# A hybrid decoder layer on one core: loads issued some steps ahead of their use, and a region of its own for the group statistics

## The chip, the core and the metric

The kernel runs on one core of a Trainium2 chip. The metric is the device time of one execution in microseconds, of which the median of several runs is compared. The engines are TensorE (PE, matmuls; its weight loads are PEld), VectorE (DVE), ScalarE (ACT), GpSimd (POOL) and SyncE (SP, which only issues transfers). Each engine works through its own list of instructions in order.

## What is computed

One layer of a decoder over 2048 prompt tokens and 32 sample tokens (8 sequences of 4), all in float32 with width 1024. Cut to what matters, the reference is:

```python
def run_layer(x, bufs, ...):
    h = rms_norm(x, norm_pre_mix)
    q, k, v, z1, z2, g_a, g_b = project_inputs(h, w_in, b_gate)
    for gi, (win, dil) in enumerate(((128, 1), (512, 4), (2048, 16))):
        # prompt: window attention over every dil-th key; sample: the same over a cache
        o, lse = dilated_group_prompt(...) if bufs is None else dilated_group_sample(..., bufs[gi], ...)
    o_a = merge_dilations(outs, lses)       # softmax over the three groups' lse
    o_b = spatial_gate(z1, z2, ...)         # gMLP in chunks of 128
    merged = g_a * (o_a @ w_ao) + g_b * (o_b @ w_bo)
    x = x + rms_norm(merged @ w_out, norm_post_mix)
    h2 = rms_norm(x, norm_pre_ffn)
    f = jnp.square(jax.nn.relu(h2 @ w_up)) @ w_down
    return x + rms_norm(f, norm_post_ffn)
```

Each head group has four heads of 64; the kernel takes them as two pairs (hp 0 and 1).

## The kernel before

**Stages.** Half s = 0 holds 1024 prompt tokens and the 32 sample tokens, half s = 1 the other 1024 prompt tokens. For each half the program goes through six groups (pair hp, dilation g): `project` computes q, k and v of the group, `attention` its scores, values and statistics. After the three groups of a pair, `merge` weights their outputs. Then come `gmlp`, `mix` (gates and the branch outputs) and `out_rows` (the output projection, both norms, and the transposed h2). The feed-forward part `ffn` follows for both halves: each of its two products is done with seven block products in place of eight, for which sums of weight blocks (`weight_sums`) and differences of h2 quarters (`differences`) are made beforehand. Matmuls on float32 data take three passes over split operands (high and low parts `wh`, `wl`), so a weight block is loaded (L248), rounded on ACT (L264) and its remainder made on POOL (L267).

**Lanes.** The gemms of `project`, `gmlp`, `mix` and `out_rows` set the pace on TensorE. Between their matmuls they step generators in four lanes: lane 0 attention and norms, lane 1 merges, the moves of h2 and the differences, lane 2 the sample attention and what follows it, lane 3 `weight_sums`, stepped each time 12000 columns have gone by. A `yield` gives control back to the gemm. This order is the program's; on top of it the framework's scheduler, with a timeline of its own, orders each engine's instructions anew by readiness and priority, so the yields guide where an instruction stands but do not fix it. Transfers issued on SP with `tc.issue_after` stay behind the named load.

**What the change touches.**

`attention`: unit u's scores go through L648, which adds the mask and takes each row's minimum, and L652, which takes the exponential and its row sum. Both statistics are written into columns 128 to 131 of `uo`, the unit buffer that also holds the group's values and is stored to `us` in DRAM at the group's end (L724 to L733). There is one `uo` for all groups, in `ov`.

`merge`: for each of eight blocks of 128 tokens, `fetch` (L737) loads the three groups' rows of `us` one block ahead of use into `junk`; L751 to L763 make the weights, L765 and L766 add the groups on POOL, and after four blocks four transposes (L772) take the sum to `oa`.

`sample_attention`: for K and again for V, 21 pieces are loaded into a few buffers (`pieces`) on SP, 3 for group 0 and 9 for each other group: from the cache (L818, L825), and the new rows from `smp` (L828); q of each group by L843 into one buffer. For each piece VectorE does a product and a reduction (K: L846, L847) or a product and an addition (V: L877, L886), with sums on POOL (L887, L889). At the end a matmul against a constant (L893) sums over the partitions; for it POOL's L889 has to be done, and its result bank is tag "t", two banks that the transposes of other work also use. Pair hp = 0 runs beside the attention of s = 0, with three buffers, and pair hp = 1 beside `mix` of s = 0, with two.

`to_h2` and `moved`: a normed block is transposed, scaled on VectorE (L342) and stored to `h2` (L345); `differences` loads quarters of h2 (two transfers) and makes four differences on VectorE (L1208 to L1211).

`weight_sums`: per quarter of a weight, four SP transfers DRAM to DRAM (L1188) and four additions by transfers that accumulate, issued on POOL (L1191).

The names in the rows are the program's: `ps`, `pt`, `pg`, `pu` are banks of PSUM, `wh`/`wl` weights, `pair`, `flat`, `oa`, `act`, `ov`, `xt`, `junk`, `gbc`, `prod`, `zs`, `e0` buffers in SBUF, `us`, `smp`, `h`, `up_sums`, `down_sums` are in DRAM, `con` are constants.

Of the kernel before, what the change touches and what calls it, by code (L numbers as in the profile page):

```python
# [18 lines left out]
P = 128  # L19
D = 1024  # L20
# [74 lines left out]
def hybrid_step(ctx: ExitStack, tc: tile.TileContext, ins: dict, outs: list):  # L95
# [372 lines left out]
    count = {"s": 0, "t": 0, "q": 0}  # L468
# [110 lines left out]
    def attention(s, hp, g, idx, q, v):  # L579
# [26 lines left out]
        uo = units_of(ov[:, A_U : A_U + 8 * UW])  # L606

# [23 lines left out]
        def scores(u):  # L631
# [6 lines left out]
            for h in range(2):  # L638
                def keys(rows):
# [61 lines left out]
        for i in range(8 + LAG_T + LAG_V):  # L701
# [14 lines left out]
            if i == 7:  # L716
                k_used.add(idx)
        dst = us[s][hp][:, g, :]
# [12 lines left out]
    def merge(s, hp):  # L731
# [9 lines left out]
        yield  # L741
        for b4 in range(2):
# [25 lines left out]
            for _ in range(4):  # L768
                yield
# [11 lines left out]
    def sample_attention(hp):  # L781
# [9 lines left out]
        else:  # L791
# [4 lines left out]
            pieces = [a0[:, 0:512], a0[:, 512:1024]]  # L796
            prods = [sm.tile([P, 512], F32, tag="e0", name="prod") for _ in range(2)]
        cnt = [0, 0]

        def nxt(lst, w):  # L800
            cnt[w] += 1
            return lst[(cnt[w] - 1) % len(lst)]
# [3 lines left out]
        scv = sc.rearrange("p (e k) -> p e k", k=KEYS)  # L806

        def steps(kv):

            cs = slice(hp * P, hp * P + P)  # L810
            for g in range(3):
                while (hp, g) not in known:
                    yield None
                if g == 0:
                    src = cache[0][:, kv, cs].rearrange("(p i) c -> p i c", i=8)
                    for hf in range(2):
                        pc = t4(nxt(pieces, 0))
                        nc.sync.dma_start(pc, src[:, hf * 4 : hf * 4 + 4, :])  # L818
                        for i in range(4):
                            yield g, hf * 4 + i, pc[:, i, :].unsqueeze(1).to_broadcast([P, 4, P])  # L820
                else:
                    src = cache[g][:, kv, cs].rearrange("(p i r) c -> p i r c", i=8, r=DIL[g])
                    for i in range(8):
                        pc = t4(nxt(pieces, 0))
                        nc.sync.dma_start(pc, src[:, i, :4, :])  # L825
                        yield g, KEY0[g] + i, pc
                pc = nxt(pieces, 0)
                nc.sync.dma_start(pc, smp_d[g][hp][1 + kv].unsqueeze(1).to_broadcast([8, 16, 512]))  # L828
                pc = t4(pc)
                if g == 0:  # L830
                    for i in range(4):
                        yield g, 8 + i, pc[:, i, :].unsqueeze(1).to_broadcast([P, 4, P])
                else:
                    yield g, KEY0[g] + 8, pc

        loaded = -1
        for item in steps(0):
            if item is None:
                yield
                continue  # L840
            g, key, rows = item
            if g != loaded:
                nc.sync.dma_start(q, smp_d[g][hp][0].unsqueeze(1).to_broadcast([8, 16, 512]))  # L843
                loaded = g
            pr = nxt(prods, 1)
            nc.vector.tensor_tensor(t4(pr), t4(q), rows, ALU.mult)  # L846
            nc.vector.tensor_reduce(scv[:, :, key], hd(pr), AX, ALU.add)  # L847
            yield
# [26 lines left out]
        for n, (g, key, rows) in enumerate(steps(1)):  # L875
# [14 lines left out]
        yield  # L890
        yield
# [191 lines left out]
    def out_rows(s, behind=None):  # L1083
# [22 lines left out]

        def norms(b):
            y, n = of(b)
# [18 lines left out]
        def moved(b):  # L1127
            y, n = of(b)
            if s == 1:
                y = sm.tile([P, D], F32, tag="x", name="xt")  # L1130
                nc.sync.dma_start(y, n1_d[b * P : (b + 1) * P])
            for _ in range(5):
                yield
            yield from to_h2(s, y, n, b * P)
# [21 lines left out]
        for b in range(n_rows):  # L1156
            y, n = of(b)
            pt = gemm_rows([(list(zip(lhs(b), pb)), 256)], n)
            copy_any(y[:, 256:512], pt)
            pt = gemm_rows([(list(zip(lhs(b), w)), 512)], n)  # L1160
            free[0] = b + 1
            copy_any(y[:, 512:], pt)
            gen = push(0, norms(b))
            if s == 0:
                free[2] = push(1, after(gen, moved(b)))
            else:
                behind(b)
        if s == 1:
            drain(0)
            return [moved(b) for b in range(n_rows)] + [differences(s)]  # L1170
# [4 lines left out]
    def weight_sums():  # L1175

        for name, dst in (("w_up", up_d), ("w_down", down_d)):
            w = ins[name][0]
            hk, hm = w.shape[0] // 2, w.shape[1] // 2
            for q in range(4):  # L1180
                n = hk // 4
                rows = slice(q * n, (q + 1) * n)
                a11, a12 = w[q * n : (q + 1) * n, :hm], w[hk + q * n : hk + (q + 1) * n, :hm]
                a21, a22 = w[q * n : (q + 1) * n, hm:], w[hk + q * n : hk + (q + 1) * n, hm:]
                s1, s2, s3, s4 = (dst[i, rows] for i in range(4))
                for to, src in ((s1, a21), (s2, a11), (s3, a11), (s4, a12)):
                    with tc.issue_after(load[0].ins):
# [443 lines left out]
```

## Time and profile before

| | us |
|---|---|
| runs, median (lowest to highest) | 2965.51 (2965.22 to 2975.41) |
| profiled execution | 2969.44 |
| span of its profile | 2967.7 |

| engine | busy us | share |
|---|---|---|
| PE | 2854.4 | 96% |
| PEld | 2588.2 | 87% |
| DVE | 1323.3 | 45% |
| ACT | 1243.7 | 42% |
| POOL | 1185.7 | 40% |

The mean granted clock of TensorE is 0.983 of its full speed. To read it: TensorE is busy nearly all the time, its weight loads overlap its matmuls, and every other engine is idle more than half of the span. The shares are averages over stages. The rows that follow come from views by stretch of time and from the timelines of single engines. In a timeline row the number in brackets is the engine's idle time ahead of the instruction, with what ended it.

### The profile page before, as it was taken

The page shows a single profiled execution, that of the slowest core. Times are in us where ns is not written, and L with a number is a line of the kernel's source. Part 1 is how long each engine was busy: PE and PEld are TensorE (multiplying, and loading weights), DVE is VectorE, ACT ScalarE, POOL GpSimd, SP SyncE. Part 2 cuts the span into 40 slices and gives each one's busy share as a digit, 9 for nine tenths or more (in the row PEclk, how much of TensorE's full clock was granted, in tenths as well). Part 3 has the DMA queues.
Part 4 walks back from the last instruction along what each step waited for, and adds up shares of the span by engine and source line. Part 5 has one row for each costly group of instructions (what it writes and reads, how often), then busy time and mean ns, then how long its engine had stood idle before and what let it go on. Part 6 is the DMA issues. An engine that isn't in the chain of part 4 may idle for free. (4 is left out here: it accounts for less than half of the span.)

```text
span 2967.7 us, 45073 instructions
## 1 busy us (share of the span) xinstructions
PE 2854.4 (96%) x17382; PEld 2588.2 (87%) x17382; DVE 1323.3 (45%) x2288; ACT 1243.7 (42%) x2457; POOL 1185.7 (40%) x883
## 2 busy tenths in 40 slices
PE   8997999889998999999999999999999999999997
PEld 7897999889987888878889899999999888878885
DVE  5668456460473435451023654353343644452323
ACT  5353452211563434541134544554344555554343
POOL 3226224253302223143332344445555744445555
PEclk9998999999999999999999999999999999999998
DMA  5635525554459454353525987576665765686654
GB/s 166 187 117 167 155 71 143 139 147 120 135 184 234 134 146 117 83 127 91 145 81 200 301 277 236 180 244 213 206 197 191 241 205 187 192 275 191 192 182 149
DMA packets 463831, 515.50 MB, mean 174 GB/s; under 512 B 25472, under 2 KB 359872, under 8 KB 454400
## 3 DMA queue, kind: packets, MB, share of 16 engines
q1 hardware_dynamic: 452528, 475.59, 50.4%
q0 software_dynamic: 10944, 36.97, 6.9%
q8 instruction: 137, 2.24, 0.3%
q14 instruction: 78, 0.64, 0.1%
q10 hardware_dynamic: 144, 0.07, 0.0%
HBM read 396.96 MB, written 182.68 MB: 195 GB/s over the span
## 5 line engine op out<-in xcount | busy, mean ns | idle before, releaser
L283 PE MATMUL pg<-act,wh 128*128 128x352 f32 (+3 forms) x3424 | 948.8, 355 | 3.3 <-DVE xt L1055 1.4
L1241 POOL TENSOR_TENSOR wf<-raw,wf 128x512 fp32r<-128x512 f32 x448 | 633.2, 1416 | 688.2 <-ACT wf L1240 647.3
L283 PEld LDWEIGHTS pg<-act,wh 128*128 128x128 f32 x3424 | 617.3, 191 | 56.0 <-DVE xt L1055 2.4
L283 PE MATMUL pg<-act,wl 128*128 128x352 f32 (+3 forms) x1712 | 605.5, 354 | 0.0
L1240 ACT CAST wf<-raw 128x512 fp32r<-128x512 f32 x448 | 277.2, 619 | 505.0 <-PE pd L1330 205.0
L267 POOL TENSOR_TENSOR wl<-raw,wh 128x1024 fp32r<-128x1024 f32 (+1 forms) x106 | 253.5, 2392 | 386.2 <-ACT wh L264 334.6
L1330 PE MATMUL pd<-act,wf 128*128 128x264 f32 x2880 | 363.0, 286 | 7.4 <-ACT act L1240 4.6
L1330 PEld LDWEIGHTS pd<-act,wf 128*128 128x128 f32 x2880 | 356.5, 190 | 8.2 <-ACT act L1240 4.8
L283 PEld LDWEIGHTS pg<-act,wl 128*128 128x128 f32 x1712 | 326.5, 191 | 26.4
L1410 PE MATMUL pe<-wf,act 128*128 128x512 f32 x1008 | 237.1, 396 | 3.9 <-POOL wf L1241 3.9
L1410 PEld LDWEIGHTS pe<-wf,act 128*128 128x128 f32 x1008 | 190.3, 189 | 49.4 <-POOL wf L1241 4.7
L264 ACT CAST wh<-raw 128x1024 fp32r<-128x1024 f32 (+1 forms) x104 | 105.4, 1013 | 275.6 <-PE pg L283 155.3
L1339 DVE TENSOR_TENSOR ov<-pd,ov 128x528 f32<-128x528 f32 x140 | 96.2, 704 | 203.8 <-PE pd L1330 203.2
L1330 PE MATMUL pd<-pair,wf 128*128 128x264 f32 x1440 | 184.6, 284 | 0.0
L1330 PE MATMUL pe<-act,wf 128*128 128x512 f32 x768 | 182.6, 392 | 0.1
L1330 PEld LDWEIGHTS pd<-pair,wf 128*128 128x128 f32 x1440 | 178.1, 188 | 0.0
L1241 DVE TENSOR_TENSOR act<-flat,act 128x1024 fp32r<-128x1024 f32 (+1 forms) x76 | 103.1, 1360 | 158.7 <-ACT act L1240 158.6
L1330 PEld LDWEIGHTS pe<-act,wf 128*128 128x128 f32 x768 | 143.8, 188 | 32.9 <-ACT pair L1240 0.3
L652 ACT ACTIVATE ov<-ov 128x256 f32<-128x256 f32 (+1 forms) x192 | 91.8, 478 | 169.8 <-DVE ov L648 168.3
L1339 DVE TENSOR_TENSOR ov<-pe,ov 128x512 f32<-128x512 f32 x136 | 91.5, 687 | 137.3 <-PE pe L1330 126.4
L1330 PE MATMUL pd<-oa,wf 128*128 128x264 f32 x1056 | 135.0, 284 | 0.1
L1330 PEld LDWEIGHTS pd<-oa,wf 128*128 128x128 f32 x1056 | 130.9, 188 | 0.4 <-DVE oa L1241 0.3
(279 smaller groups left out, 4183.7 us busy)
## 6 DMA issues: line engine op xcount, KB each, us to landing
raw<-in_w_in_dram SPq DMA_DIRECT2D x84, 512.0 KB
raw<-up_sums SPq DMA_DIRECT2D x128, 256.0 KB
raw<-down_sums SPq DMA_DIRECT2D x128, 256.0 KB
flat<-f SPq DMA_DIRECT2D x48, 528.0 KB
raw<-in_w_up_dram SPq DMA_DIRECT2D x96, 256.0 KB
raw<-in_w_down_dram SPq DMA_DIRECT2D x96, 256.0 KB
flat<-f SPq DMA_DIRECT2D x48, 512.0 KB
f<-ov SPq DMA_DIRECT2D x16, 1056.0 KB
```

Of the source, the lines that this page charges most:

```text
L264: nc.scalar.copy(wh[:, :o], raw[:, :o])
L267: eng.tensor_tensor(wl[:, :o], raw[:, :o], wh[:, :o].bitcast(F32), ALU.subtract)
L283: nc.tensor.matmul(pt[:, :n], a[:, o : o + P], b, start=(i == 0 and j == 0), stop=(i == last and j == 2))
L652: nc.scalar.activation(pb[:, h, :w], pb[:, h, :w], AF.Exp, scale=-1.0, bias=uo[:, u, 128 + h : 129 + h], accum_out=uo[:, u, 130 + h : 131 ...
L1240: nc.scalar.copy(high, raw)
L1241: eng.tensor_tensor(low, raw, high.bitcast(F32), ALU.subtract)
L1330: nc.tensor.matmul(pt[:, o : o + n], w[:, a], x[:, b, c : c + n], start=first and j == 0, stop=last and j == 2)
L1339: nc.vector.tensor_tensor(X[to], res, X[add], ALU.add)
L1410: nc.tensor.matmul(pts[t], x[k][:, c, t * P : (t + 1) * P], w[:, d, 0], start=k == 0 and j == 0, stop=k == 15 and j == 2)
```

## The change

All changes are in how far ahead of its use data is asked for.

1. `attention` writes the row minima and sums to `stats`, a region of its own in `ov` with two buffers that take turns, and a GpSimd copy at step 9 puts them into `uo`. There are twelve such copies, one for each group of each half.
2. `merge` has four steps after its first fetch, two per block, and six ahead of the transposes (before: one, one, four).
3. `sample_attention` lists its loads and issues them as many pieces ahead as there are buffers; pair 1 has four buffers (two more in `ov`); q of group 1 has a buffer of its own; four steps stand ahead of the first use and five ahead of the last matmul (before: two).
4. `moved` is one generator over all blocks, paced by the norms, with two steps per half block.
5. `weight_sums` issues the loads of one quarter interleaved with the additions of the quarter before.
6. `differences` has four steps between load and use (before: one).

The core of the diff:

```diff
+    A_M = A_T + 1024
...
         uo = units_of(ov[:, A_U : A_U + 8 * UW])
+        stats = units_of(ring("m", A_M, 32, 2))
...
                     pb[:, h, :w], sp[:, h, :w], mask[:, 2 * P - w : 2 * P], 1.0, 3.0e38, ALU.add, ALU.min,
-                    uo[:, u, 128 + h : 129 + h],
+                    stats[:, u, h : h + 1],
...
-                    pb[:, h, :w], pb[:, h, :w], AF.Exp, scale=-1.0, bias=uo[:, u, 128 + h : 129 + h],
-                    accum_out=uo[:, u, 130 + h : 131 + h],
+                    pb[:, h, :w], pb[:, h, :w], AF.Exp, scale=-1.0, bias=stats[:, u, h : h + 1],
+                    accum_out=stats[:, u, 2 + h : 3 + h],
...
                 k_used.add(idx)
+            if i == 9:
+                nc.gpsimd.tensor_copy(uo[:, :, P:], stats)
...
         m3_next = fetch(0)
-        yield
+        for _ in range(4):
+            yield
...
                 yield
-            for _ in range(4):
+                yield
+            for _ in range(6):
                 yield
...
-            pieces = [a0[:, 0:512], a0[:, 512:1024]]
+            pieces = [a0[:, 0:512], a0[:, 512:1024], row(3)[:, 0:512], row(3)[:, 512:1024]]
...
+        qs = [q, U, q]
+        def load_q(g):
+            nc.sync.dma_start(qs[g], smp_d[g][hp][0].unsqueeze(1).to_broadcast([8, 16, 512]))
...
         def steps(kv):
+            todo, n = loads(kv), len(pieces)
+            issued = 0
+            for i, (g, _, shared, keys) in enumerate(todo):
+                while True:
+                    while issued < min(len(todo), i + n) and (hp, todo[issued][0]) in known:
+                        gi, src = todo[issued][:2]
+                        pc = pieces[issued % n]
+                        if kv == 0 and (issued == 0 or gi != todo[issued - 1][0]):
+                            load_q(gi)
+                        nc.sync.dma_start(t4(pc) if len(src.shape) == 3 and src.shape[2] == P else pc, src)
+                        issued += 1
+                    if issued > i:
+                        break
+                    yield None
+                if i == 0:
+                    for _ in range(4):
+                        yield None
+                pc = t4(pieces[i % n])
+                for j, key in enumerate(keys):
+                    yield g, key, pc[:, j, :].unsqueeze(1).to_broadcast([P, 4, P]) if shared else pc
...
-        yield
-        yield
+        for _ in range(5):
+            yield
         pu = ps.tile([P, 512], F32, tag="t", name="pt")
...
         def norms(b):
+            for _ in norm_steps(b):
+                paces[0] += 1
+                yield
...
-        def moved(b):
+        def moved():
+            for b in range(n_rows):
+                y, n = of(b)
+                if s == 1:
+                    y = sm.tile([P, D], F32, tag="x", name="xt")
+                    nc.sync.dma_start(y, n1_d[b * P : (b + 1) * P])
+                    for _ in range(4):
+                        yield
+                for _ in range(3):
+                    if paces[0] < 4 * (b + 1) + 2:
+                        yield
+                while paces[0] < 4 * (b + 1):
+                    yield
+                for _ in to_h2(s, y, n, b * P):
+                    yield
+                    yield
...
+            return ((s1, a21, a22), (s3, a11, a21), (s2, a11, s1), (s4, a12, s2))
+        before = None
+        for name, dst in (("w_up", up_d), ("w_down", down_d), (None, None)):
+            for q in range(4 if name else 1):
+                now = parts(name, dst, q) if name else None
+                for i in range(4):
+                    if now:
+                        with tc.issue_after(load[0].ins):
+                            nc.sync.dma_start(now[i][0], now[i][1])
+                        yield
+                    if before:
+                        nc.gpsimd.dma_start(before[i][0], before[i][2], accum_op=ALU.add, max_dma_last_dim=8192)
+                        yield
+                before = now
...
             nc.sync.dma_start(l, h2_d[s][k + 4])
-            yield
+            for _ in range(4):
+                yield
```

`loads(kv)` lists the transfers of the cache pieces and the new rows that stood in `steps` before, in the same sequence.

What the change does to the order of instructions stands here at three places. A row gives line, operation and what it writes from what it reads; lines of the changed program are some 2 to 40 higher.

VectorE, around the first scores of the second attention group of s = 0. Before, sample products (L846) and reductions (L847) stand ahead of the first score of the group (L648):

```order
L847 TENSOR_REDUCE xt<-ov 128x8 x2
L628 TENSOR_TENSOR oa<-flat_147,oa 64x256
L846 TENSOR_TENSOR ov<-xt,ov 128x512
L177 COPY ov<-pu 128x128
L847 TENSOR_REDUCE xt<-ov 128x8
L846 TENSOR_TENSOR ov<-xt 128x512
L846 TENSOR_TENSOR ov<-xt,ov 128x512
L847 TENSOR_REDUCE xt<-ov 128x8 x2
L522 COPY smp<-pg 128x32
L846 TENSOR_TENSOR ov<-xt,ov 128x512
L648 ISA ov<-ps,con 128x128
```

The same place of the changed program (L650 is the score, L858 the sample product, L561 a copy that stands five rows ahead of the piece above):

```order
L561 COPY st<-pt 32x384
L650 ISA ov<-ps,con 128x128
L650 ISA ov 128x1
L177 COPY ov<-pu 128x128
L177 COPY ov<-pt 128x512
L650 ISA ov<-ps,con 128x128
L650 ISA ov 128x1
L650 ISA ov<-ps,con 128x256
L650 ISA ov 128x1
L630 TENSOR_TENSOR oa<-flat_147,oa 64x256
L858 TENSOR_TENSOR ov<-xt 128x512
L858 TENSOR_TENSOR ov<-xt,ov 128x512
```

Three scores moved ahead of the sample products of this stretch.

SyncE, at the start of the sample attention of pair 1, before (L818 and L825 cache pieces, L828 new rows, L843 q, L248 weights, L1188 weight sums):

```order
L818 DMA gbc<-in_cache_kv_w_dram 128x4x128 x2
L248 DMA raw<-in_w_ao_dram 128x2x128
L248 DMA raw<-in_w_bo_dram 128x4x128
L1188 DMA up_sums<-in_w_up_dram 128x2048
L248 DMA raw<-in_w_in_dram 128x8x128
L828 DMA gbc<-smp_104 128x1x512
L248 DMA raw<-in_w_in_dram 128x8x128
L1188 DMA up_sums<-in_w_up_dram 128x2048
L825 DMA gbc<-in_cache_kv_w_dram 128x4x128
L843 DMA junk<-smp_106 128x1x512
L825 DMA gbc<-in_cache_kv_w_dram 128x4x128
```

The same place of the changed program (L842 all pieces, L811 q, L1228 weight sums):

```order
L842 DMA gbc<-in_cache_kv_w_dram 128x4x128 x2
L248 DMA raw<-in_w_in_dram 128x8x128
L811 DMA junk<-smp_104 128x1x512
L842 DMA ov<-smp_104 128x1x512
L842 DMA ov<-in_cache_kv_w_dram 128x4x128
L811 DMA o_4935<-smp_106 128x1x512
L248 DMA raw<-in_w_ao_dram 128x2x128
L248 DMA raw<-in_w_bo_dram 128x4x128
L1228 DMA up_sums<-in_w_up_dram 128x2048
L248 DMA raw<-in_w_in_dram 128x8x128
L842 DMA gbc<-in_cache_kv_w_dram 128x4x128
```

The new rows, the first piece of group 1 and its q moved ahead of three weight loads; the pieces alternate between `gbc` and `ov`.

VectorE, at the end of the sample attention of pair 1, before (L877 products, L899 the scaling that reads what the matmul L893 wrote):

```order
L877 TENSOR_TENSOR junk<-gbc,zs 128x512
L877 TENSOR_TENSOR prod<-gbc,zs 128x512
L886 TENSOR_TENSOR prod<-prod,junk 128x512
L877 TENSOR_TENSOR prod<-gbc,zs 128x512
L899 TENSOR_TENSOR prod<-pt,rl 8x512
```

The same place of the changed program (L895 products, L1071 and L1073 the additions of the gates' gemms in `mix`, L917 the scaling behind the matmul L911):

```order
L895 TENSOR_TENSOR prod<-ov,zs 128x512
L895 TENSOR_TENSOR junk<-ov,zs 128x512
L904 TENSOR_TENSOR prod<-prod,junk 128x512
L895 TENSOR_TENSOR prod<-gbc,zs 128x512
L1071 TENSOR_TENSOR xt<-xt,ps 128x352
L1073 TENSOR_TENSOR xt<-xt,pg 128x352
L1071 TENSOR_TENSOR xt<-xt,ps 128x352
L915 RECIPROCAL rl<-ps 8x8
L917 TENSOR_TENSOR prod<-pt,rl 8x512
```

Three additions of `mix` and the reciprocal moved between the last product and the scaling.

## Rows read from the trace of the kernel before

**Rows 1.** Windows: us, busy (instructions) of each engine, PEclk, DMA share, GB/s.

```profile
200.00:300.00 100.00, 83.71 (x507) 77.71 (x507) 83.14 (x208) 41.10 (x123) 54.75 (x48) 0.89 0.50 143
500.00:600.00 100.00, 88.72 (x533) 87.83 (x532) 51.27 (x76) 23.37 (x37) 32.17 (x22) 0.93 0.55 148
...
900.00:1000.00 100.00, 91.04 (x492) 76.27 (x492) 40.62 (x83) 32.28 (x75) 27.14 (x21) 0.97 0.85 232
...
1300.00:2968.00 1668.00, 1638.30 (x9880) 1463.15 (x9880) 640.82 (x767) 718.57 (x1161) 777.52 (x526) 0.99 0.62 197
```

**Rows 2.** TensorE's timeline: start, us, line, out<-in, shape, count, [idle before <-releaser].

```profile
144.32 0.47 PE L646 MATMUL ps<-pair,oa 128*128 128x128 f32 x1 [5.95 <-DVE ov L648]
...
288.50 1.86 PE L893 MATMUL pt<-xt,con 128*8 128x512 f32 x2 [4.79 <-DVE el L756]
...
548.95 0.90 PE L283 MATMUL ps<-oa,wh 128*128 128x320 f32 x2 [10.05 <-DVE xt L1053]
...
618.71 0.56 PE L283 MATMUL ps<-oa,wh 128*128 128x320 f32 x2 [2.65 <-DVE xt L1053]
...
650.80 1.88 PE L893 MATMUL pt<-o,con 128*8 128x512 f32 x2 [7.64 <-POOL o L889]
...
924.23 0.43 PE L326 MATMUL ps<-con,flat 32*128 32x32 f32 x4 [1.79 <-DVE h L342]
...
940.42 0.39 PE L646 MATMUL ps<-pair,oa 128*128 128x256 f32 x1 [1.02 <-DVE ov L648]
...
957.23 0.39 PE L646 MATMUL ps<-pair,oa 128*128 128x256 f32 x1 [3.45 <-DVE ov L648]
...
960.64 0.55 PE L646 MATMUL ps<-pair,oa 128*128 128x256 f32 x1 [2.09 <-DVE ov L648]
```

**Rows 3.** Windows around the half clock that follows those pieces (columns of Rows 1).

```profile
142.00:148.80 6.80, 4.48 (x17) 4.43 (x18) 4.42 (x10) 1.74 (x6) 0.60 (x1) 0.50 0.96 249
...
285.30:302.40 17.10, 13.48 (x52) 11.38 (x53) 12.31 (x49) 8.19 (x24) 6.16 (x11) 0.50 0.61 182
...
541.30:555.00 13.70, 6.05 (x21) 6.05 (x22) 9.06 (x12) 0.78 (x1) 4.11 (x3) 0.50 0.86 210
619.80:623.20 3.40, 3.40 (x13) 3.01 (x11) 1.87 (x3) 0.15 (x1) 2.63 (x1) 0.51 0.31 91
647.10:654.00 6.90, 3.20 (x7) 1.50 (x8) 1.37 (x2) 0.11 (x1) 2.92 (x2) 0.51 0.55 142
...
957.80:964.60 6.80, 4.71 (x14) 3.52 (x13) 6.20 (x13) 2.17 (x9) 2.48 (x3) 0.50 0.99 210
```

**Rows 4.** VectorE's timeline, rows that waited for a transfer.

```profile
132.41 0.69 DVE L846 TENSOR_TENSOR ov<-xt 128x512 f32<-128x512 f32 x1 [5.42 <-DMA xt<-smp]
...
286.23 0.16 DVE L751 TENSOR_REDUCE lo<-junk 128x2 f32<-128x6 f32 x1 [4.03 <-DMA junk<-us]
...
528.04 1.42 DVE L846 TENSOR_TENSOR prod<-junk,gbc 128x512 f32<-128x512 f32 x2 [6.28 <-DMA gbc<-in_cache_kv_w_dram]
...
648.65 0.69 DVE L877 TENSOR_TENSOR prod<-gbc,zs 128x512 f32<-128x512 f32 x1 [3.05 <-DMA gbc<-smp]
...
956.12 0.71 DVE L1208 TENSOR_TENSOR xt<-xt 128x528 f32<-128x528 f32 x1 [7.16 <-DMA xt<-h]
```

**Rows 5.** Timelines of POOL and DVE at 243; POOL's group of L627 by shape.

```profile
242.99 2.38 POOL L267 TENSOR_TENSOR wl<-raw,wh 128x1024 fp32r<-128x1024 f32 x1
...
243.05 2.86 DVE L877 TENSOR_TENSOR xt<-ov,xt 128x512 f32<-128x512 f32 x1
...
L627 POOL CAST oa<-flat 64x256 fp32r<-64x256 f32 x96 | 46.5, 485 | 178.9 <-PE ps L646 122.3 <-PE ps L647 41.3 <-ACT flat L507 12.6
```

**Rows 6.** TensorE's timeline in 240:270, stalls behind L648 (columns of Rows 2).

```profile
240.38 0.33 PE L646 MATMUL ps<-pair,oa 128*128 128x128 f32 x1 [1.89 <-DVE ov L648]
...
268.81 0.58 PE L646 MATMUL ps<-pair,oa 128*128 128x256 f32 x1 [3.01 <-DVE ov L648]
```

**Rows 7.** Waits of SP's queue: line, releaser: us in total, times, longest us.

```profile
SPq L248 <- POOL wl L267: 643.7, 81, 24.2
```

More of the change, by code (lines that the diff above doesn't have):

```diff
@@ L467, in hybrid_step @@
     A_T = A_V + 2048
-    count = {"s": 0, "t": 0, "q": 0}
+    A_M = A_T + 1024
+    count = {"s": 0, "t": 0, "q": 0, "m": 0}
     k_used = set()
@@ L806, in sample_attention, with loads @@
         scv = sc.rearrange("p (e k) -> p e k", k=KEYS)
-        def steps(kv):
+        qs = [q, U, q]
+        def load_q(g):
+            nc.sync.dma_start(qs[g], smp_d[g][hp][0].unsqueeze(1).to_broadcast([8, 16, 512]))
+        def loads(kv):
             cs = slice(hp * P, hp * P + P)
+            out = []
             for g in range(3):
-                while (hp, g) not in known:
-                    yield None
                 if g == 0:
                     src = cache[0][:, kv, cs].rearrange("(p i) c -> p i c", i=8)
[L816 to L820, printed above, removed]
+                    for i in (0, 4):
+                        out.append((g, src[:, i : i + 4, :], True, range(i, i + 4)))
                 else:
@@ L823, in steps @@
                     for i in range(8):
[L824 to L834, printed above, removed]
@@ L836, in sample_attention @@
-        loaded = -1
-        for item in steps(0):
-            if item is None:
-                yield
[L840 to L847, printed above, removed]
+                        out.append((g, src[:, i, :4, :], False, (KEY0[g] + i,)))
@@ new lines, in loads, with steps @@
+                new = smp_d[g][hp][1 + kv].unsqueeze(1).to_broadcast([8, 16, 512])
+                out.append((g, new, g == 0, range(8, 12) if g == 0 else (KEY0[g] + 8,)))
+            return out
+        def steps(kv):
+            todo, n = loads(kv), len(pieces)
[18 more added lines that the diff above has]
+                    yield g, key, pc[:, j, :].unsqueeze(1).to_broadcast([P, 4, P]) if shared else pc
@@ L848, in sample_attention @@
+        for n, item in enumerate(steps(0)):
+            if item is not None:
+                g, key, rows = item
+                pr = prods[n % 2]
+                nc.vector.tensor_tensor(t4(pr), t4(qs[g]), rows, ALU.mult)
+                nc.vector.tensor_reduce(scv[:, :, key], hd(pr), AX, ALU.add)
             yield
@@ L874, in sample_attention @@
         firsts, pair_sum = [prods[0], prods[1]], None
-        for n, (g, key, rows) in enumerate(steps(1)):
+        n = -1
+        for item in steps(1):
+            if item is None:
+                yield
+                continue
+            n += 1
+            g, key, rows = item
             pr = U if n == 0 else q if n % 2 == 0 else firsts[n // 2 % 2]
@@ L1162, in out_rows @@
             copy_any(y[:, 512:], pt)
[L1163 to L1166, printed above, removed]
+            push(0, norms(b))
+            if s == 1:
                 behind(b)
+            elif b == 0:
+                free[2] = push(1, moved())
         if s == 1:
             drain(0)
-            return [moved(b) for b in range(n_rows)] + [differences(s)]
+            return [moved(), differences(s)]
         push(1, differences(s))
```

35 lines of the change are left out of this document (9 added, 26 removed).

## The prediction

> **What bounds the kernel now.** I read the stretches first [rows 1]: from 1300 us on TensorE is busy 1638.3 of 1668.0 us, so nothing outside TensorE can give much there, and the feed-forward part keeps its time. The loss lies in the first 1300 us, in the attention, merge and mix stages: 83.71 busy in 200:300, 88.72 in 500:600, 91.04 in 900:1000. Then I went down TensorE's timeline for the single idle pieces in those stretches [rows 2]: each row ends with the idle time ahead of the matmul and the instruction that released it. Every one of the large ones is released by VectorE or GpSimd, none by a weight. Third, I looked at the granted clock around them [rows 3]: after each of these idle pieces the rows show 0.50 or 0.51, which is 1.2 GHz, where the stretch would otherwise run at 2.4 GHz; TensorE's busy time in such a window is twice what it would be, so half of it is lost as well. Last, VectorE's timeline [rows 4] tells why VectorE was late: it executes in order, and an instruction ahead of the one that TensorE wanted stood waiting for a transfer. 132.41 (a product of the sample attention, waiting 5.42 us for `smp`) stands ahead of the scores' L648 that releases 144.32; 286.23 (the merge's L751, 4.03 us for `junk<-us`) stands ahead of the L311 that frees the bank for L893 at 288.50; 528.04 (6.28 us for a cache piece) is the longest of several such waits that hold back L1053; 648.65 (3.05 us for `smp`) is the last product, from which L889 and then L893 follow; 956.12 (7.16 us for the h2 quarter of L1208) stands ahead of the scores of the second half. So the bound is TensorE, and what can be won is idle TensorE behind VectorE behind a transfer that was issued too late.
>
> **The change part by part.** Each term is the idle time in [rows 2] and half of TensorE's busy time in its window of [rows 3], against the profiled execution of 2969.44 us.
>
> Group statistics (L648, L652 to a region of their own). What it moves: the first instruction of a group that touches the unit buffer is now a GpSimd copy some steps later, and the order of the changed program puts the scores of the second group ahead of the sample products (first excerpt), so TensorE's 144.32 no longer hangs on 132.41. Gain 5.95 + 4.48/2 = 8.2 us. I take all of it.
>
> Sample pieces of the second pair of heads (L846, L877). There are four buffers in place of two, and q per group has a buffer of its own. In SP's order the next group's q now stands ahead of weights that it followed before (second excerpt). The stall at 548.95 gives 10.05 + 6.05/2 = 13.1, that at 618.71 gives 2.65 + 3.40/2 = 4.4: 17.5 us in all. The transfer of a piece itself is unchanged and its wait was up to 6.28 us, about two products with their reductions; a lead of two more pieces covers that. I take all of it. For the first pair of heads the number of buffers stays at three, so there I take nothing beyond the term above.
>
> The sum over samples (L893, now L911, behind five steps). At 650.80 TensorE's matmul stood right behind L889; in the changed order three additions of the next gemm (L1071, L1073, L1071) lie between the last product and what follows L911 (third excerpt), and the wait gets TensorE work in front of it. Gain 7.64 + 3.20/2 = 9.2 us, all taken.
>
> Merge rows (L737, more steps between fetch and use). The stall at 288.50 is 4.79 + 13.48/2 = 11.5 us. In the changed program's order the fetch still follows the store `us<-ov` on SP with the first use about as close as before, because the scheduler closes the steps up; so VectorE's wait stays, and only TensorE's dependence on it (L893 behind L311) may go, since L911 is some steps later. Between 0 and 11.5 I take three quarters, 8.6.
>
> Quarters of h2 and their transposes (`moved`, `differences`). The four stalls of 924 to 961 are 1.79 + 1.02 + 3.45 + 2.09 = 8.35, with 4.71/2 the sum is 10.7 us. In the changed order the transposes (L342) stand among the norms and no longer in one run ahead of the scores, and the first two quarters' differences come earlier, but the last two still stand among the scores. Half: 5.4 us.
>
> Weight sums. The additions on the GpSimd queue get their loads a quarter earlier. No stall of [rows 2] is released by them, so I count 0. If that cover were thinner than it looks, GpSimd's cast L627 and correction L267, which are queued behind them, would be late for TensorE.
>
> What it adds. Twelve GpSimd copies of 128x8x4. The nearest row is GpSimd's cast L627, 485 ns at 64x256 [rows 5]; twelve are 12 x 0.485 = 5.8 us on GpSimd, whose 40% of busy time has room. Queued behind each copy are L627 and L267, which TensorE's operands need. As bounds: 0 when TensorE has work in front, 5.8 when every copy is passed on. I take 0, and keep 5.8 for the range.
> On VectorE there is a side price. A product L877 takes 2.86 us from 243.05, where L267 has occupied GpSimd since 242.99 for 2.38 us; both end within 0.6 us of each other [rows 5]. The Trainium skill ("SBUF — State Buffer", section "SBUF: two separate sides") says that VectorE with two SBUF inputs and GpSimd take one shared port pair by an exclusive lock, and the loser blocks for the other's whole instruction; the row agrees, and by that rule each copy could hold VectorE as long as it holds GpSimd, which makes the sum up to 5.8 us worse and speaks against the copies.
>
> A shifted order. Other scores may now stand behind other waits. The nearest rows are the stalls of 240 to 269 behind L648, four of them with 1.89, 2.23, 0.97 and 3.01, 8.1 us in all [rows 6], which shows the first and the last; the change doesn't aim at these. New ones could be from 0 to that again with some clock, 11 us. I take 8.
>
> Sum: 8.2 + 17.5 + 9.2 + 8.6 + 5.4 - 8 = 40.9, so 2969.44 - 40.9 = 2928.5 for an execution like the profiled one. That lies 3.9 above the median of the runs (2965.51), which with the same gain gives 2924.6: **2925 us**.
>
> **The rivals.** First, every late transfer goes: the terms in full are 8.2 + 17.5 + 9.2 + 11.5 + 10.7 = 57.1, and the four stalls of 240 to 269 with half of their clock loss, some 11 us, go too: 68, or 2897 us. For it: they all have one cause. Against: the order of merge and differences is half unchanged.
> Second, the change doesn't do what it says: the scheduler sets the order by its own reckoning, and pieces issued earlier in the program land no earlier because SP stands in front of them. SP's wait at L248 for a free weight buffer adds up to 643.7 us in 81 waits, the longest 24.2 [rows 7], longer than any wait of VectorE in [rows 4]. Then only the first term and half of the merge's remain, 8.2 + 5.7 = 13.9: 2951.6 us.
> Third, on the other side: SP is in order, and with a ring of four it issues a piece as soon as one is free, so it can stand waiting for VectorE to give back a piece with weight loads L248 queued behind it. Between the first and the last piece of the second pair there are 21 such loads. It decides once such a wait is longer than the lead that SP has with weights, 643.7/81 = 7.9 us. VectorE's longest wait there was 6.28, so most weights stay covered; if half of the 21 come late by 4 us, which is what a late piece cost VectorE on the rows (3.05 to 6.28), 42 us of stall stand against 13.9 won: 2994 us, and TensorE's rows would show L283 released by L264 or L267.
>
> **How the numbers follow.** Forecast (2905 to 2945) 0.52; all goes (below 2905) 0.13; undone by the scheduler (2945 to 2965) 0.25; SP held up (over 2980) 0.10. About 0.5%, 15 us, is what a measurement of this kernel can tell from no change: faster means below 2950.7. Of the second rival's quarter about a third lies below that. Faster 0.52 + 0.13 + 0.08 = 0.73; the same 0.17; slower 0.10. The range goes from the first rival's 2897 less 4 us, the distance between the profiled execution and the median, to 2962, which takes in the second rival and the 5.8 us of the copies; the forecast's own range is 2905 to 2945.
>
> **What would show it.** In the profile of the changed kernel: the row of TensorE's scores near 144 has no idle time of 6 us; no L283 near 549 and 619 waits for VectorE's L1071; L911 has no idle time of 7 us ahead of it; busy time in 500:600 and 600:700 goes from 89 to above 95, and 900:1000 from 91 to 95. The windows at half clock there vanish with the stalls. The merge's L751 (now L755) still waits for `junk<-us`. Wrong would be the forecast if VectorE's waits for pieces are as long as before, if the same stalls stand at other lines (VectorE ahead of the scores), or if L283 waits for weights.

## The result, and the profile after

The changed kernel takes 2937.05 us (median; 2935.09 to 2949.5), before 2965.51 (2964.21 to 2975.41), five runs of each: ratio 0.9903, 95% interval 0.9877 to 0.9929, which is 28.8 us less, a gain of 1.0% where 40.5 us were forecast. The profiled execution's span fell from 2967.7 to 2933.4. The page of after, its first lines (busy us, share, instructions):

```profile
span 2933.4 us, 45117 instructions
PE 2846.6 (97%) x17382; PEld 2582.9 (88%) x17382; DVE 1333.0 (45%) x2288; ACT 1244.4 (42%) x2456; POOL 1189.6 (41%) x895
```

TensorE runs the same 17382 matmuls. Its idle time went from 2967.7 - 2854.4 = 113.3 to 86.8 us, and its busy time fell by 7.8 because less of it lies at half clock (mean granted clock 0.983 before, 0.990 after): 26.5 + 7.8 = 34.3, which is the difference of the spans. By stretch of 100 us (columns of Rows 1), against [rows 1]:

```profile
200.00:300.00 100.00, 87.37 (x562) 80.02 (x563) 88.58 (x221) 41.30 (x123) 55.81 (x52) 0.98 0.58 160
...
500.00:600.00 100.00, 96.39 (x587) 95.21 (x586) 55.02 (x75) 24.81 (x38) 42.05 (x28) 0.98 0.56 149
600.00:700.00 100.00, 95.88 (x574) 94.08 (x573) 36.28 (x42) 18.33 (x33) 44.93 (x29) 0.97 0.50 135
700.00:800.00 100.00, 94.79 (x636) 90.95 (x635) 40.67 (x63) 44.85 (x100) 31.25 (x17) 0.97 0.50 153
...
900.00:1000.00 100.00, 98.21 (x541) 83.98 (x540) 47.91 (x113) 40.35 (x109) 25.84 (x27) 0.97 0.57 162
```

500:600 rose from 88.72 to 96.39 and 900:1000 from 91.04 to 98.21, as foretold; 700:800 fell, and it was near full before (98.78). TensorE's timeline of after, at the places of [rows 2]:

```profile
136.96 0.63 PE L696 MATMUL pu<-ov 128*128 128x64 f32 x4 [2.27 <-DVE ov L177]
...
590.78 0.56 PE L283 MATMUL ps<-oa,wh 128*128 128x320 f32 x2 [1.45 <-DVE xt L1071]
595.85 0.59 PE L283 MATMUL pg<-act,wh 128*128 128x352 f32 x2 [2.00 <-DVE xt L1073]
623.28 0.43 PE L283 MATMUL ps<-oa,wl 128*128 128x352 f32 x1 [2.10 <-POOL wl L267]
636.90 0.43 PE L283 MATMUL pg<-act,wl 128*128 128x352 f32 x1 [2.02 <-POOL wl L267]
...
788.55 1.11 PE L326 MATMUL ps<-con,ov 128*128 128x128 f32 x4 [3.99 <-DVE ov L1146]
...
920.12 0.39 PE L648 MATMUL ps<-pair,oa 128*128 128x256 f32 x1 [1.70 <-DVE ov L650]
```

The stalls of 5.95, 4.79, 10.05, 2.65 and 7.64 us are gone. In their place stand smaller ones, and one that is new, at 788. The half clock, a granted clock of 0.50, follows them (columns as above):

```profile
596.50:599.90 3.40, 3.40 (x14) 3.40 (x13) 3.40 (x5) 0.00 (x0) 2.39 (x2) 0.50 0.75 221
623.80:627.20 3.40, 3.40 (x14) 3.40 (x13) 1.10 (x2) 0.00 (x0) 2.87 (x2) 0.50 0.48 133
637.50:640.90 3.40, 3.40 (x14) 3.24 (x14) 2.39 (x2) 0.19 (x1) 3.40 (x4) 0.50 0.96 194
787.60:794.40 6.80, 5.84 (x25) 5.66 (x26) 6.62 (x11) 2.75 (x9) 0.00 (x0) 0.50 0.29 80
```

### The profile page after: what moved, and what is told of

Read it like the earlier page. It is cut to its first block, busy times and chain, and to the rows that moved or that the text cites. A ratio compares the mean times of both kernels' runs of the same rounds, so it can differ in the third digit from the quotient of the medians.

```text
span 2933.4 us, 45117 instructions
## 1 busy us (share of the span) xinstructions
PE 2846.6 (97%) x17382; PEld 2582.9 (88%) x17382; DVE 1333.0 (45%) x2288; ACT 1244.4 (42%) x2456; POOL 1189.6 (41%) x895
## 5 line engine op out<-in xcount | busy, mean ns | idle before, releaser
L283 PE MATMUL pg<-act,wh 128*128 128x352 f32 (+3 forms) x3424 | 944.9, 354 | 2.9 <-DVE xt L1073 2.0
L283 PEld LDWEIGHTS pg<-act,wh 128*128 128x128 f32 x3424 | 614.3, 191 | 52.5 <-DVE xt L1073 2.3
L283 PE MATMUL pg<-act,wl 128*128 128x352 f32 (+3 forms) x1712 | 605.0, 354 | 2.0 <-POOL wl L267 2.0
L267 POOL TENSOR_TENSOR wl<-raw,wh 128x1024 fp32r<-128x1024 f32 (+1 forms) x106 | 252.6, 2384 | 362.3 <-ACT wh L264 320.2
L283 PEld LDWEIGHTS pg<-act,wl 128*128 128x128 f32 x1712 | 325.8, 190 | 28.8 <-POOL wl L267 2.3
L1381 DVE TENSOR_TENSOR ov<-pd,ov 128x528 f32<-128x528 f32 x140 | 96.4, 705 | 201.5 <-PE pd L1372 200.8
L1381 DVE TENSOR_TENSOR ov<-pe,ov 128x512 f32<-128x512 f32 x136 | 91.5, 688 | 137.4 <-PE pe L1372 126.4
```

Of the source, the lines that this page charges most:

```text
L267: eng.tensor_tensor(wl[:, :o], raw[:, :o], wh[:, :o].bitcast(F32), ALU.subtract)
L283: nc.tensor.matmul(pt[:, :n], a[:, o : o + P], b, start=(i == 0 and j == 0), stop=(i == last and j == 2))
L1381: nc.vector.tensor_tensor(X[to], res, X[add], ALU.add)
```

## The experiments

**Theory:** each part takes away its own stall of TensorE, and the prices add up. **Main rival:** any edit shifts the scheduler's order, and the gain is that of another order. Each time is given as its ratio to the kernel before, from runs on the same chip, and, to compare, as that ratio times 2965.5. The whole change was timed in five runs, and with the two intervals combined a difference between it and another row is uncertain by some 9 us. In plain medians the three fastest rows (2933.9, 2933.3 and 2931.4 us) lie 3 to 6 us below the whole change's 2937.05, and not the 10 or 11 of the last column.

| kernel | ratio (interval) | us against before |
|---|---|---|
| the whole change | 0.9903 (0.9877 to 0.9929) | -28.8 |
| statistics alone | 0.9988 (0.9977 to 1.0) | -3.6 |
| samples alone | 0.9977 (0.9964 to 0.9989) | -6.8 |
| merge alone | 0.9974 (0.9961 to 0.9988) | -7.7 |
| h2 alone | 0.9991 (0.998 to 1.0002) | -2.7 |
| sums alone | 0.9988 (0.9978 to 0.9998) | -3.6 |
| all but statistics | 0.9940 (0.9923 to 0.9958) | -17.8 |
| all but samples | 0.9950 (0.9933 to 0.9966) | -14.8 |
| all but h2 | 0.9866 (0.9846 to 0.9887) | -39.7 |
| all but h2, additions pinned | 0.9881 (0.9863 to 0.9898) | -35.3 |
| all but moves | 0.9869 (0.9853 to 0.9886) | -38.8 |
| all but h2 and sums | 0.9913 (0.9898 to 0.9927) | -25.8 |
| whole, moves later | 0.9866 (0.985 to 0.9883) | -39.7 |

**Statistics alone.**

```diff
+        stats = units_of(ring("m", A_M, 32, 2))
-                    uo[:, u, 128 + h : 129 + h],
+                    stats[:, u, h : h + 1],
+            if i == 9:
+                nc.gpsimd.tensor_copy(uo[:, :, P:], stats)
```

> The kernel before with the statistics region alone. Theory (each part takes away its own stall, and the stalls' prices add up): TensorE's idle 5.95 us at 144 goes and nothing else does, 8 us with its clock, 2957 us; the stalls at 288, 549, 618, 650 and 924 to 961 stand as before. Rival one (the gain of the whole is that of a shifted order, which any edit would give in another amount): somewhere within 15 us of before, with stalls at other places and L648's own stall not the one that is missing. Rival two (the twelve copies cost as much as they give): 2965, GpSimd's casts L629 later, stall at 144 gone and others of 1 to 3 us new behind L629.

2.44 us stand where 5.95 stood, so the stall at 144 shrank; but the gain is 3.6 us (0 to 6.8 by the interval) and not 8. The merge's wait now holds back a score at 289 (VectorE's row, then TensorE's):

```profile
288.37 0.16 DVE L755 TENSOR_REDUCE lo<-junk 128x2 f32<-128x6 f32 x1 [7.07 <-DMA junk<-us]
...
289.42 0.58 PE L648 MATMUL ps<-pair,oa 128*128 128x256 f32 x1 [4.66 <-DVE ov L650]
```

The wait of [rows 4] stayed, and what stands behind it on VectorE was another instruction. The later casts of rival two are not what is late here.

**Samples alone.**

```diff
-            pieces = [a0[:, 0:512], a0[:, 512:1024]]
+            pieces = [a0[:, 0:512], a0[:, 512:1024], row(3)[:, 0:512], row(3)[:, 512:1024]]
+        qs = [q, U, q]
-        yield
-        yield
+        for _ in range(5):
+            yield
         pu = ps.tile([P, 512], F32, tag="t", name="pt")
```

> The kernel before with the sample attention's part alone: loads as many pieces ahead as there are buffers, four buffers for pair 1, q of group 1 in a buffer of its own, five steps ahead of the last matmul. Theory: the stalls at 549 and 618 (17.5 us with clock) and at 650 (9.2) go, that at 288 (11.5) in part, less the smaller ones that the whole change shows in their place at 591, 596, 623 and 637 (7.6 us of idle time): 2965 - 27 + 8 - 4 = some 2942; the stall at 144 stays. Rival one (a shifted order): gain below 10 us. Rival two (this part is the whole change): 2937.

6.8 us, a third of the 23 expected. The stall at 549 is halved and not gone, and behind it is again a late piece, the last one: it was issued at 530.42 and used 8.6 us later (rows of TensorE, SP and VectorE, and two windows):

```profile
544.04 0.90 PE L283 MATMUL ps<-oa,wh 128*128 128x320 f32 x2 [5.76 <-DVE xt L1065]
...
529.19 0.76 SPq L1200 DMA_DIRECT2D up_sums<-in_w_up_dram  x1
530.42 0.60 SPq L836 DMA_DIRECT2D gbc<-smp  x1
...
538.98 2.46 DVE L852 TENSOR_TENSOR prod<-junk,gbc 128x512 f32<-128x512 f32 x1 [4.81 <-DMA gbc<-smp]
...
500.00:520.00 20.00, 20.00 (x127) 20.00 (x126) 19.79 (x27) 3.77 (x6) 9.20 (x6) 1.00 1.04 259
520.00:540.00 20.00, 18.28 (x114) 17.99 (x112) 11.05 (x18) 5.40 (x8) 4.13 (x3) 1.00 0.94 272
```

The DMA engines were full (1.04 and 0.94), with a load of the weight sums of 1 MB right ahead of this piece of 256 KB. In the whole change the same piece is issued at 514.76 and used 4.6 us later. Part of the rest was lost elsewhere: 500:700 won 8.6 us of busy time (178.24 to 186.83), but in 100:250 the granted clock of the profiled execution is 0.94, before 0.97; a stall of 1.63 us at 178 that wasn't there has 6.8 us of half clock beside it. A gain below 10 us is what rival one had, too; its account is tested below.

**Merge alone.**

```diff
         m3_next = fetch(0)
-        yield
+        for _ in range(4):
+            yield
```

> The kernel before with the merge's additional steps alone. Theory: the scheduler closes the steps up, VectorE's wait for junk<-us stays near 47.7 us and the time within 4 us of before; if the L893 at 288 still stands behind L751, its 4.79 us stay. Rival: the steps do move the use away from the load, VectorE's wait for junk<-us falls below 30 us and the stall at 288 goes: 2954.

VectorE's wait for the rows stays nearly as long, as the theory has it (its waits: us, times, longest; the whole change has 44.8 in 19):

```profile
DVE lo L752 <- DMA junk<-us: 42.9, 18, 6.3
```

but the time falls by 7.7 us, as the rival has it: in 280:300 no stall of TensorE is over 1.06 us. At this place the use did move away from the load: VectorE waits 0.97 us where it waited 4.03.

```profile
289.19 0.16 DVE L752 TENSOR_REDUCE lo<-junk 128x2 f32<-128x6 f32 x1 [0.97 <-DMA junk<-us]
```

So the waits keep their sum, and the one that mattered is gone; a wait of 5.2 us now stands at 311, where no stall of TensorE reaches 1 us.

**h2 alone.**

```diff
-                free[2] = push(1, after(gen, moved(b)))
+            elif b == 0:
+                free[2] = push(1, moved())
-            yield
+            for _ in range(4):
+                yield
```

> The kernel before with the moves of h2 and the differences alone (earlier transposes, four steps between load and use of the quarters). Theory: the four stalls of 924 to 961 go to about a quarter, 8 us with clock, and the new wait that the whole change shows at 788 (3.99 us of TensorE ahead of a transpose for the norm's L1146, with 6.8 us at half clock) comes: net 0 to -4, 2961 to 2966. Rival: the wait at 788 comes from the other parts, not from this one: 2956.

2.7 us, in the theory's range and outside the rival's; but there is no stall at 788, as the rival has it, so that one needs the company of another part. It stands in all but statistics (4.32 us at 802) and in all but samples (3.40 us at 809) as well, so neither of these two is needed. Of the stalls of 924 to 961 one of 5.83 us at 953.60 is the only one left over 1.3 us, more than the quarter of the theory.

**Sums alone.**

```diff
+            return ((s1, a21, a22), (s3, a11, a21), (s2, a11, s1), (s4, a12, s2))
+                    if before:
+                        nc.gpsimd.dma_start(before[i][0], before[i][2], accum_op=ALU.add, max_dma_last_dim=8192)
```

> The kernel before with the weight sums' new order alone (loads of one quarter interleaved with the additions of the quarter before). Theory: no stall of TensorE was released by them, so within 4 us of before, though GpSimd's waits ahead of these transfers, 92 and 86 us before, should fall. Rival (a late addition holds GpSimd's L267 and L627 and so TensorE): GpSimd's waits fall by more than half and the time by 5 to 10 us.

3.6 us, as the theory has it. GpSimd's waits fell from 92.1 and 86.3 us to 82.4 and 67.2, not by half.

**All but statistics** (the whole change less the edit of the first experiment).

> The whole change with the statistics back in the unit buffer (no copies, no region). Theory: 8 us more than the whole change, 2945, with an idle piece of some 6 us at 144 ahead of L646 and its half clock. Rival (shifted order): no difference that can be told, 2933 to 2941, with no stall over 3 us at 144.

11.0 us are lost; the 8 expected lie within the uncertainty, and the time is outside the rival's range. TensorE has a stall of 3.51 us at 144, and another score waits for GpSimd, on which L627 stood behind a correction L267 of 2.78 us:

```profile
144.22 0.48 PE L646 MATMUL ps<-pair,oa 128*128 128x128 f32 x1 [3.51 <-DVE ov L648]
...
275.14 0.53 PE L646 MATMUL ps<-pair,oa 128*128 128x256 f32 x1 [4.72 <-POOL oa L627]
```

The stall at 144 alone would decide nothing, for a kernel that has the statistics' region, all but h2, shows 3.62 us at 145. VectorE's rows tell what the region does. Before, and here, the group's first score waits for the store of the unit buffer (before, then all but statistics):

```profile
143.97 0.29 DVE L648 CUSTOM_DVE_ANT_0 ov<-ps,con 128x128 f32<-128x128 f32 x1 [1.38 <-DMA us<-ov]
...
143.86 0.29 DVE L648 CUSTOM_DVE_ANT_0 ov<-ps,con 128x128 f32<-128x128 f32 x1 [2.02 <-DMA us<-ov]
```

With the region the group's scores run from 123.84 on in the whole change, and the wait for the store passes to the first copy of values into the buffer (L177 on VectorE; the whole change, then all but h2, and there TensorE's score behind it):

```profile
142.97 0.29 DVE L177 COPY ov<-pu 128x128 f32<-128x128 f32 x1 [1.16 <-DMA us<-ov]
...
144.64 0.29 DVE L177 COPY ov<-pu 128x128 f32<-128x128 f32 x1 [1.58 <-DMA us<-ov]
...
145.28 0.30 PE L648 MATMUL ps<-pair,oa 128*128 128x128 f32 x1 [3.62 <-DVE ov L650]
```

**All but samples** (the whole change less the edit of the second experiment).

> The whole change with the sample attention as before (two buffers for pair 1, two steps ahead of its last matmul). Theory: the stalls of 10.05, 2.65 and 7.64 us at 549, 618 and 650 come back with their half clock, some 27 us, less the 7.6 us of smaller ones at 591 to 637 and their clock: 2955 to 2960. Rival (a shifted order is what helps): below 2948, with no stall over 5 us between 500 and 660.

14.0 us are lost, to 0.9950, which is 2950.7: short of the theory's 2955 and above the rival's 2948. The three stalls are back, as the theory has it:

```profile
537.93 0.90 PE L283 MATMUL ps<-oa,wh 128*128 128x320 f32 x2 [10.65 <-DVE xt L1059]
...
609.42 0.90 PE L283 MATMUL ps<-oa,wh 128*128 128x320 f32 x2 [5.38 <-DVE xt L1059]
...
642.48 1.87 PE L899 MATMUL pt<-o,con 128*8 128x512 f32 x2 [8.62 <-POOL o L895]
```

**All but h2** (the whole change less the edit of the fourth experiment).

> The whole change with the moves of h2 and the differences as before. Theory: the wait of 3.99 us at 788 and its half clock go (7 us won), the four stalls of 924 to 961 come back (8.35 us and clock, 8 lost): within 4 us of the whole change. Rival: the moves are worth 6 us or more in this company, 2943 or above.

Neither: it is 11 us faster than the whole change, with intervals that overlap a little (0.9877 against 0.9887), and the next two kernels ask what in this part costs. There is no stall at 788:

```profile
700.00:800.00 100.00, 98.81 (x686) 95.28 (x685) 39.59 (x62) 44.75 (x101) 33.74 (x19) 1.00 0.52 152
```

**All but moves** (all but h2, with the differences' four steps).

> The change without the moves of h2, but with the four steps between load and use of the quarters in the differences. Theory: the 11 us that the part on h2 costs lie in the moves alone (the transposes ahead of the first norm at 788), so this one is within 4 us of the change without both, 2930 to 2938, without a stall near 790. Rival: the differences cost it, 2941 or more.

0.9869: the differences cost nothing that can be told from these runs; what costs is the moves.

**Whole, moves later.**

```diff
-                for _ in range(3):
-                    if paces[0] < 4 * (b + 1) + 2:
-                        yield
-                while paces[0] < 4 * (b + 1):
+                while paces[0] < 4 * min(b + 3, n_rows):
                     yield
```

> The whole change with one edit in the moves of h2: a block's transposes are paced two blocks of norms later, so that the first ones no longer stand right behind the first norm's L1146. Theory (the moves cost their 11 us by the wait at 788, where TensorE's transposes stand ahead of a norm that itself waited for its load of x): the 3.99 us and the half clock behind them go, 7 to 8 us, the shorter stalls of the second half's scores at 920 stay: 2927 to 2933 on the scale where the whole change has 2937. Rival (the moves cost by something else, such as VectorE's L342 and L1250 among the first scores of the second half): the stall at 788 goes and the time stays, 2937 within 4.

0.9866, 10.9 us better than the whole change. The stall at 788 is gone with its half clock (700:800 is 98.79 busy at clock 1.00, where the whole change has 94.79 at 0.97), some 7 us. In 900:1000 a part is given back, for a score stands behind a later quarter of h2:

```profile
700.00:800.00 100.00, 98.79 (x678) 94.67 (x678) 38.99 (x62) 45.85 (x104) 31.55 (x18) 1.00 0.51 153
...
915.35 0.58 PE L648 MATMUL ps<-pair,oa 128*128 128x256 f32 x1 [4.77 <-DVE ov L650]
```

So the wait at 788 is shown as a cost of the moves; that it is all of their 11 us is not. Another part stands in the feed-forward, where TensorE waits for VectorE's additions L1381, and these stand behind the differences (the whole change):

```profile
1735.51 6.05 PE L1372 MATMUL pd<-act,wf 128*128 128x264 f32 x48 [0.97 <-DVE ov L1381]
...
1780.08 7.60 PE L1372 MATMUL pd<-act,wf 128*128 128x264 f32 x48 [2.05 <-DVE ov L1381]
```

With 0.83 us at 1757 these are 3.9 us; with the moves later 2.5 are left, the kernel before has 1.8 and all but h2 none. An interval of a quarter of a per cent can't split the sum further.

**All but h2 and sums.**

> The change without the part on h2 and without the sums' new order. Theory: in the sample attention alone the DMA engines were busy 1.04 and 0.94 of 500:520 and 520:540 with four transfers of 1 MB for the sums among the pieces, the last piece came 8.5 us after its issue and 5.76 us of TensorE at 544 stayed; with the old order of the sums this comes back: 2940 to 2945. Rival (the sums' order is worth nothing, as alone): 2934 within 4.

13.9 us are lost against all but h2 (some 7 either way), as the theory has it, though the sums alone gave 3.6. The stall is back at 534.73; the windows of this kernel, and under them the loads and additions of the sums (SP and POOL):

```profile
534.73 0.90 PE L283 MATMUL ps<-oa,wh 128*128 128x320 f32 x2 [6.79 <-DVE xt L1071]
...
500.00:520.00 20.00, 20.00 (x126) 20.00 (x125) 12.80 (x19) 3.84 (x8) 6.34 (x4) 1.00 0.99 262
520.00:540.00 20.00, 13.21 (x72) 12.92 (x71) 12.73 (x22) 3.69 (x5) 5.01 (x4) 0.83 0.89 241
...
495.85 2.40 SPq L1206 DMA_DIRECT2D up_sums<-in_w_up_dram  x1
520.17 0.72 SPq L1206 DMA_DIRECT2D up_sums<-in_w_up_dram  x1
...
505.94 0.81 POOL L1209 DMA_DIRECT2D up_sums<-in_w_up_dram  x1 [3.14 <-DMA up_sums<-in_w_up_dram]
528.40 0.81 POOL L1209 DMA_DIRECT2D up_sums<-up_sums  x1 [15.14 <-PE pg L283]
```

Between 490 and 530 five transfers of 1 MB start beside the pieces here, the four shown and an addition at 490.44; the last piece, issued at 521.36, is used at 529.51. In all but h2 one load (496.07) and one addition (503.90) start before its last piece is used at 524.60. The new order of the sums spaces them out.

**Additions pinned** (all but h2, each addition queued on GpSimd behind the last L267).

```diff
+                        with tc.issue_after(load[1].ins):
+                            nc.gpsimd.dma_start(before[i][0], before[i][2], accum_op=ALU.add, max_dma_last_dim=8192)
```

> The change without the part on h2, and each addition of the weight sums queued on GpSimd behind the weight correction L267 that the program had last issued, so that the scheduler can't move it up to stand right behind its own load (in the whole change it starts 6 to 9 us after the load that precedes it). Theory: the new order of the sums does not happen in the whole change because the scheduler moves the additions up; pinned, GpSimd's waits for them fall from 118 us to below 30, the weight L267 is no longer late and the 3.44 us of TensorE at 629 with its half clock go: 7 us less than without the pin, 2927 us. Rival (the transfers themselves are what is in the way, not their place on GpSimd): waits fall and the time stays, 2934.

In the whole change each of the 32 additions still starts 6 to 11 us behind its own load, the scheduler having moved it up to there (SP, then POOL):

```profile
625.28 0.58 SPq L1228 DMA_DIRECT2D up_sums<-in_w_up_dram  x1
...
633.67 0.81 POOL L1231 DMA_DIRECT2D up_sums<-up_sums  x1 [6.80 <-DMA up_sums<-in_w_up_dram]
```

Pinned, GpSimd has no wait for a sum's load any more and the stall at 629 is gone, but 0.9881 is no better than 0.9866: the rival's outcome. Other stalls came; a piece was 6.25 us late at 519.52, and that the load and the addition of 501.17 and 508.05 made it so is likely, not shown:

```profile
536.73 0.56 PE L285 MATMUL ps<-oa,wh 128*128 128x320 f32 x2 [3.48 <-DVE xt L1073]
```

**What follows.** Taking the samples or the sums out brings their own named stalls back (538, 609 and 642; 535), so the main rival falls as an account of these two. For the statistics the rows show the wait that the region moves, but not that all of the 11.0 us are its own. And the prices don't add up as the theory had it: alone the five parts make 24.4 us, and out of company 11.0 (statistics), 14.0 (samples), 13.9 (sums) and -11 (h2), each within 7 to 10 us. Merge was not taken out of the whole, so its price in company stays open.

## Why the prediction was right in direction and too large

The bound was read rightly: TensorE behind VectorE behind a late transfer. The time is in the range and 12 us above the forecast. By its steps:

- **Statistics, 8.2:** 11.0 in company, within 9; alone 3.6, since the merge's wait takes hold of a score then. The scores did move ahead of the sample products. But two readings were off. What VectorE's score waited for last at 143.97 was the store `us<-ov`, not the product's transfer, which had only made that store late. And the first instruction of a group that touches the unit buffer is not the GpSimd copy but the copy of the values L177, which now waits for that store.
- **Samples and the sum over them, 17.5 + 9.2:** mis-sized, 14.0 (within 9). The three stalls went, and four smaller ones came: 1.45 + 2.00 + 2.10 + 2.02 = 7.6 us, with half of 10.2 us at half clock, 5.1. So 26.7 - 12.7 = 14.0; that it meets the measured number to the digit is luck. The step that failed is "I take all of it": VectorE's products of the next pieces now stand in front of L1071 and L1073, and a weight's L267 is late behind GpSimd's sums of the samples (623) and behind an addition of the weight sums that waited 6.80 us for its load (637).
- **Merge, 8.6:** 7.7 alone. Right in size, and VectorE's waits do keep their sum (44.8 us). The reason given, that L911 stands some steps later, is not needed: merge alone lacks these steps, and there the wait ahead of L893 went itself.
- **h2, 5.4:** the failed step. The part costs some 11 us by the ratios, 3 by the medians. The idle time of 900:1000 shrank by 7 us, as foretold, but half of that came without this part (5.41 us are idle there in all but h2, 8.96 before). And the transposes L326, now right behind the first norm, hold TensorE for that norm's L1146. ScalarE, in order, had stood 5.43 us on the next half's rows of x with this norm's square root L360 behind it, and then VectorE waited for the store of the norm's own x1 out of the rows that L1146 overwrites (after, ScalarE and VectorE):

```profile
785.32 0.63 ACT L356 ACTIVATE junk<-xt 128x512 f32<-128x512 f32 x1 [5.43 <-DMA xt<-in_x_prompt_dram]
...
785.95 0.28 ACT L360 ACTIVATE sd<-ss,half 128x1 f32<-128x1 f32 x1
...
787.75 0.75 DVE L1146 TENSOR_SCALAR ov<-ov,rs 128x1024 f32<-128x1024 f32 x1 [1.33 <-DMA x<-ov]
```

  The step looked at what the transposes free and not at what they wait for.
- **Weight sums, 0:** also failed. They are worth 13.9 beside the samples, within 7. No stall in [rows 2] is *released* by them, but they fill the DMA engines in front of the pieces that are.
- **A shifted order, 8 lost:** it can't be told apart; the new stalls at 137, 591 to 637 and 788 are 13.8 us of idle time, with clock more; the 7.6 of 591 to 637 are counted above already.

The second rival (the scheduler undoes the change) holds for the additions of the sums, and for the sum of the merge's waits. The third did not happen as put: L283 does wait for L267 twice, 2.1 and 2.0 us, behind GpSimd's queue and not SP's.

A shared port shows once more, ahead of the stall at 136.96, where a sample product takes four times its usual 0.69 us (after, GpSimd and VectorE):

```profile
133.50 2.57 POOL L267 TENSOR_TENSOR wl<-raw,wh 128x1024 fp32r<-128x1024 f32 x1 [1.40 <-ACT wh L264]
...
133.77 2.85 DVE L858 TENSOR_TENSOR ov<-xt,ov 128x512 f32<-128x512 f32 x1
```

The Trainium skill ("SBUF — State Buffer", "SBUF: two separate sides") calls this an exclusive lock between VectorE with two SBUF inputs and GpSimd; these rows agree.

## What to carry to other kernels

Price a stall with the follower that it leaves: when the late transfer is cured, the next late thing in the same stretch decides, and here that took back some 12.7 of 26.7 us. Where a change moves work earlier, ask what that work itself waits for, since on an engine that works in order an early instruction is a wait for all behind it. Parts that share the DMA engines can't be priced one at a time: the sums' order was worth 3.6 us alone and 13.9 beside the samples.

Three versions beat both kernels: all but h2, all but moves, and the whole with the moves two blocks later (0.9866 to 0.9869 of the kernel before). That they beat the whole change rests on the three together, since each interval overlaps its own.

## What the runs showed of the hardware that was not expected

The same piece of 256 KB took 4.6 us from issue to use in the whole change and 4.5 in all but h2, with no 1 MB transfer right ahead of it; it took 8.6 us in samples alone and 8.2 in all but h2 and sums, where one had been issued 1.2 us ahead. The DMA engines' share was not much different, 0.93 (after, 500:520) and 0.94 (samples alone, 520:540). By these four rows a transfer's lead has to be counted against what is queued with it, and not against its own size; that was not in the prediction.
